# A list schedule's latency towards matmuls, the place of a norm, and the order of small loads in a decoder layer

## The chip, the cores and the metric

The kernel runs on one core of a Trainium2 chip. The metric is the device time of one execution in microseconds (us). One execution of the kernel before was profiled; all rows below come from it. TensorE (PE) does matmuls, PEld stands for its weight loads, VectorE is DVE, ScalarE is ACT, GpSimd is POOL and SyncE is SP; SP issues nearly all DMAs.

## The reference

One decoder layer over 1024 tokens of width 1024, one sequence, float32:

```python
mod = (silu(c) @ w_ada + b_ada)            # shift1, scale1, gate1, shift2, scale2, gate2
h = rms_norm(x, norm1) * (1 + scale1) + shift1
proj = h @ w_in                            # q, k and v of three attention branches, gates, convolution inputs
mix = concat(nsa_attention(...), bgate * conv(cgate * u)) @ w_out
x = x + gate1 * mix
h2 = rms_norm(x, norm2) * (1 + scale2) + shift2
ff = square(relu(h2 @ w_ff1)) @ w_ff2      # width 4096
return x + gate2 * ff
```

The attention has eight heads of 64 and adds three branches (compressed, selected, window), each with its own softmax and a relative-position bias.

## The kernel before

Activations lie transposed: width on the partitions (eight slices, index k or c), tokens along the free axis, in two halves of 512 (hf 0 and 1). For precision each operand of a product is split into a rounded high part and a low rest, and every product is three matmuls (`mm3`): high by high, high by low, low by high. A weight tile is therefore loaded by DMA, cast (`copy`, L336 on ACT, L338 on DVE, L340 on POOL) and subtracted (`sub`, L347) before TensorE can use it. Matmuls are recorded at L312, transposes at L315, `stt` at L358, activations at L330, DMAs at L397.

The program is written twice into a plan: everything up to the second norm is one plan (`P.issue()` after `first_half`, attention and output projection), the MLP is the second. `Plan` collects operations with their costs and dependencies and works out an order by list scheduling in eight passes: `_longest` gives each operation the longest way to the end, `_forward` simulates the engines and the DMA queue and takes, on each engine, the ready operation with the highest priority, and `_backward` gives new priorities from the schedule so found. `LAT` holds the time in ns that passes between an operation on one engine and a dependent one on another. `AHEAD` gives a named group of operations a lead in priority. The order of each engine is the order of the best pass. Within a plan it is fixed; where the second plan's instructions fall among the first's on an engine is left to the framework, so some of the MLP's weight loads are issued before the first plan ends.

The stages, in order of the code:

- The group `silu`: loads of c (`ct`), `ident`, `b_ada` (`bad`) and `norm1` (`n1`), the sigmoid of c, its spread over the partitions (`dg`, two matmuls into `fa_t`, copies to `sc`), and `c1` from `bad` and `n1`. Between them stand the 16 loads of x.
- The first product (groups `stat0`, `stat1`, `first0` to `first7`): squares of x summed by matmuls into `stb` and `po`, `rsqrt_neg2` (three activations, two corrections by `stt`). For each k: two rows of w_ada (512 KB each) are multiplied with silu(c) and accumulated on DVE (128x1024), `a1` comes from that, x is multiplied, scaled and split for both halves, and 18 matmuls (three column groups, two halves, three each) follow, 144 in all.
- Compression, keys, values, queries, tables; then attention in units, with fillers for TensorE: the convolution, the output projection and the norm of the first half (`first_half`), and 30 (`NFF`) of the 32 tiles of w_ff1 for the first half. `put_hid` squares their result in one of five rotating buffers, the cells of `z_t`, `t1_t` and `cg_t`, and stores it to `d_hid` in DRAM.
- The output projection of the second half (`out_proj`, 192 matmuls): `done_second` adds the result to x1 and the squares into `sacc`. Then the second norm: the row sum (matmul into `stb`), `rsqrt_neg2`, and `norm2_apply` for eight k.
- The MLP in four chunks (`ch`) of eight tiles: `load_w` loads and splits a tile of w_ff1 into two rotating buffers `ws_r`; the first half comes from `d_hid` where it is stored and from `ff1(j, 0, w)` where not (tiles 30 and 31, in the last chunk), the second half from `ff1(j, 1, w)`; then w_ff2. A tile of `ff1` is 24 matmuls of 512 columns. Temporaries rotate over four buffers `tmp`.

Of the kernel before, what the change touches and what calls it, by code (L numbers as in the profile page):

```python
# [33 lines left out]
def f32(ap):  # L34
    return ap.bitcast(F)
# [11 lines left out]
class Plan:  # L47
# [6 lines left out]

    PASSES = 8

    LAT = {("ACT", "ACT"): 150, ("ACT", "DVE"): 142, ("ACT", "PE"): 260, ("ACT", "POOL"): 159,
           ("DVE", "ACT"): 128, ("DVE", "DVE"): 127, ("DVE", "PE"): 254, ("DVE", "POOL"): 155,
           ("PE", "ACT"): 197, ("PE", "DVE"): 196, ("PE", "PE"): 0, ("PE", "POOL"): 220,
           ("POOL", "ACT"): 180, ("POOL", "DVE"): 170, ("POOL", "PE"): 203, ("POOL", "POOL"): 102}  # L60

    def __init__(self, tc):
        self.tc, self.nc = tc, tc.nc
# [91 lines left out]
    def _forward(self, prio):  # L155

        ops = self.ops
        prio = [prio[o] for o in ops]
        npred, ready = {o: len(o.preds) for o in ops}, {o: {a[0]: max((t + self._lat(p, o, e, a[0]) for p, e, t in o.past), default=0.0) for a in o.alts} for o in ops}
        free = dict(self.free)  # L160
        heaps, pend = ({e: [] for e in self.eng} for _ in range(2))
        done, order, hw, dma, last, cold, port = bytearray(len(ops)), [], 0.0, 0.0, self.free["PE"], 0.0, 0.0

        def push(o):
            for i, (e, _, _) in enumerate(o.alts):
                heapq.heappush(pend[e], (ready[o][e], prio[o.idx], o.idx, i))

        def arrive(e, t):
            h, p = heaps[e], pend[e]
            while p and p[0][0] <= t:  # L170
                _, pr, idx, i = heapq.heappop(p)
                if not done[idx]:
                    heapq.heappush(h, (pr, idx, i))

        for o in ops:
            if not npred[o]:
                push(o)
        while len(order) < len(ops):
            best = None
            for e in self.eng:  # L180
                h, p = heaps[e], pend[e]
                while h and done[h[0][1]]:
                    heapq.heappop(h)
                while p and done[p[0][2]]:
                    heapq.heappop(p)
                arrive(e, free[e])
                t = free[e] if h else p[0][0] if p else None
                if t is not None and (best is None or t < best[0]):
                    best = (t, e)
            t, e = best  # L190
            free[e] = t
            arrive(e, t)
            if e in ("DVE", "POOL") and port > t:
                h, held = heaps[e], []
                while h and e in ops[h[0][1]].port:
                    held.append(heapq.heappop(h))
                    while h and done[h[0][1]]:
                        heapq.heappop(h)
                first = heapq.heappop(h) if h else None
                for x in held:  # L200
                    heapq.heappush(h, x)
                if first is None:
                    free[e] = min(port, pend[e][0][0]) if pend[e] and pend[e][0][0] > t else port
                    continue
                _, idx, i = first
            else:
                _, idx, i = heapq.heappop(heaps[e])
            o, cost = ops[idx], ops[idx].alts[i][1]
            if e in o.port:
                port = t + cost  # L210
            done[idx] = 1
            if not o.nbytes:
                if e == "PE":
                    if t - last > 2500:
                        cold = t + 4000
                    cost *= 2 if t < cold else 1
                    last = t + cost
                end = free[e] = t + cost
            else:
                if e == "SP":  # L220
                    hw = max(hw, t) + cost
                    start = hw + 650
                else:
                    free[e] = t + cost
                    start = t + cost + 660
                end = dma = max(dma, start) + o.nbytes * o.weight / 360.0
                end += 1000.0
                if e == "SP":
                    free[e] = max(t + 50, hw - cost, dma - 2500)
            order.append((t, o, i, end))  # L230
            for s in o.succs:
                for c in ready[s]:
                    ready[s][c] = max(ready[s][c], end + self._lat(o, s, e, c))
                npred[s] -= 1
                if not npred[s]:
                    push(s)
        return order
# [194 lines left out]


H0, H1, WR, RAN = 0, 8192, 16384, 16384 + 11328
AHEAD = {}
FA1N, FA2N = 13316, 10752

NFF = 30
# [3 lines left out]
def hymba_layer(ctx: ExitStack, tc: tile.TileContext, xT, cT, w_first, w_cols, w_vg, w_ada, w_ada2, b_ada,  # L442
                norm1, norm2, qn, kn, pe, cw1, cw2, conv_w, rel_bias, onehot, ident_c, pair_c, w_out,
                w_ff1, w_ff2, out, dbg=None):
# [32 lines left out]
    d_q = [[dtile(f"d_q{p}{i}", 2, 128, 2, 2, 256) for i in range(2)] for p in range(4)]  # L477
    d_k = [dtile(f"d_k{g}", 128, KW0 + T) for g in range(2)]
    d_v = [dtile(f"d_v{g}", 128, 8, 2, 128) for g in range(2)]
    d_hid = [dtile(f"d_hid{j}", 128, 512) for j in range(NFF)]  # L480
    d_row = dtile("d_row", NH, TROW)
    d_tab = [dtile(f"d_tab{i}", 128, TROW) for i in range(NH)]

# [591 lines left out]
    def first_half():  # L1075

        (ca, t2), (ta, tb) = cg_t, t1_t
        t_r = Rot([z[:, 0:512] for z in z_t] + [t2, tb])

        def done(c, a):  # L1080
            x = x1h[c]
            P.dma(x, xT[c, :, 0:512])
            P.stt(x, a, mod[:, 16 + c:17 + c], x, mult, add)
            add_square(c, ta, ca, x)

        tmp = Rot([ca, ta, tb])
        for k in range(8):
            load_mix(0, k, tmp(), h0[0][:, k], h0[1][:, k])
        tiles = [(w_out[c], lambda a, c=c: done(c, a)) for c in range(8)]
        yield from products([tiles[0:2], *([t] for t in tiles[2:6]), tiles[6:8]], fwx_r, h0)  # L1090
        P.zero(f32(bones), 1.0 / 1024)
        P.dma(n2, norm2)
        P.ts(a2, mod[:, 32:40], 1.0, -0.5, add, mult)
        P.tt(a2, a2, n2, mult)
        st = fa_r()
        P.mm(st, f32(bones), ca, True, True)
        y = rsqrt_neg2(ta, tb, st)
        for k in range(8):
            norm2_apply(k, t_r(), x1h[k], y, h0)
            yield  # L1100
        t_r = Rot(t_r.t + [ca])
        rot = fwx_r

        def put_hid(j, a):
            t = t_r()
            P.act(t, a, AF.Relu)
            P.act(t, t, AF.Square)
            P.dma(d_hid[j], t)

        tiles = [(w_ff1[j], lambda a, j=j: put_hid(j, a)) for j in range(NFF)]  # L1110
        P.group = "ff"
        yield from products([tiles[0:2], *([t] for t in tiles[2:])], rot, h0)

# [44 lines left out]

    x1 = [[FA1[:, 1024 * c + 512 * hf:1024 * c + 512 * hf + 512] for hf in range(2)] for c in range(8)]
    h2 = [h[0], h[1]]  # L1160
    tmp, sacc, y1 = Rot(at0), Gr(512), Gr(512)
    wt_r = Region(RA, RAN - 4160, RAN).rot(4, 2, 512)
    for c in range(8):
        P.dma(x1[c][1], xT[c, :, 512:1024])
# [6 lines left out]
    for k in range(4):  # L1171
        load_mix(1, k, [ada_acc, *ada_r.t][k], h[1][0][:, k], h[1][1][:, k])
    out_proj(wt_r, h[1], Rot(sc_t), done_second)
    P.mm(stb, f32(bones), sacc, True, True)
    rsqrt_neg2(y1, tmp(), stb)
    for k in range(8):
        norm2_apply(k, tmp(), x1[k][1], y1, h[1])
    for c in range(8):
        P.dma(x1[c][0], x1h[c])
    P.issue()  # L1180
# [13 lines left out]
    with ExitStack() as pf:  # L1194
        ff = pool(pf, "ff", side="right")
        psd = pool(pf, "psD", space=PSUM)
        banks = Rot([psd.tile([128, 512], F, name=f"pd{i}") for i in range(8)])
        Fr = Region(FA1, 8192, FA1N)
        ws_r = Fr.rot(2, 8, 128)
        tmp, ff_acc = Fr.rot(4, 512), Fr(512)  # L1200
        w5 = [Region(RA, c, c + 1024)(8, 128) for c in (*range(RAN - 4160, RAN - 1023, 1024), WR)]
        wh_r, wl_r = Rot([w5[0], w5[2], w5[4]]), Rot([w5[1], w5[3]])
        Wr = Region(RA, WR + 1024, RAN - 4160)
# [14 lines left out]
        def ff1(j, hf, w):  # L1218
# [5 lines left out]
            P.act(t, t, AF.Square)  # L1224
            split_hid(j, hf, t)

        for ch in range(4):
            for j in range(8):
                w = load_w(w_ff1[ch * 8 + j])
                if ch * 8 + j < NFF:  # L1230
                    t = tmp()
                    P.dma(t, d_hid[ch * 8 + j])
                    split_hid(j, 0, t)
                else:
                    ff1(j, 0, w)
                ff1(j, 1, w)
            if ch == 0:
                for i in range(2):
                    ada_cols(40 + 4 * i, 4, tmp, ff_acc, banks())
            for c in range(8):  # L1240
                w = load_w(w_ff2[ch, c])
                for hf in range(2):
                    a = banks()
                    for k in range(8):
                        hh = [hid[i][k][hf] for i in range(2)]
                        mm3(a, w, hh, S_[:, k], S_[:], k == 0, k == 7)
                    P.stt(x1[c][hf], a, mod[:, 40 + c:41 + c], x1[c][hf], mult, add)
                    if ch == 3:
                        P.dma(out[c, :, hf * 512:hf * 512 + 512], x1[c][hf])
# [82 lines left out]
```

## Time and profile before

| | |
|---|---|
| median of 3 runs | 1369.71 us (1368.28 to 1371.58) |
| the profiled execution | 1369.85 us |
| its span, first to last instruction | 1368.1 us |
| TensorE busy | 1326.0 us, 97% |
| VectorE busy | 777.8 us, 57% |
| ScalarE busy | 623.2 us, 46% |
| mean granted clock of TensorE | 0.986 |
| read from and written to HBM | 145.48 and 32.61 MB |

The time is a little longer than the span, by what lies around the instructions. Shares are averages over stages that have different limits. TensorE's matmuls are pipelined and their ends are modelled, so TensorE can be shown busy while it runs below its pace: the number of matmuls in a stretch tells more than its busy share.

### The profile page before, as it was taken

What the parts mean: (1) busy time and instruction counts of PE and PEld (TensorE: products, weight loads), DVE (VectorE), ACT (ScalarE), POOL (GpSimd) and SP (SyncE); (2) the same over time, 40 slices, a digit from 0 to 9 for tenths busy, and PEclk for the clock granted to TensorE, in tenths of its full rate; (3) what the DMA queues carried; (4) which work ended last, traced back from release to release, by engine and by line L of the source; (5) the groups of instructions that cost most, each with busy time, mean ns of one, the idle gap of its engine ahead of it and who ended that gap; (6) DMA issues with size and microseconds to landing.
All of it is one profiled execution on the core that took longest, in us unless ns stands there. A gap on an engine that the chain in (4) does not pass through costs nothing.

```text
span 1368.1 us, 18289 instructions
## 1 busy us (share of the span) xinstructions
PE 1326.0 (97%) x6424; PEld 1080.7 (79%) x6424; DVE 777.8 (57%) x1882; ACT 623.2 (46%) x1293; POOL 134.9 (10%) x240
## 2 busy tenths in 40 slices
PE   5899999999999999999999988999999999999998
PEld 2679788887878788888888866888888888888887
DVE  5987886878686886566565557443422442143222
ACT  5766653777564786565666344310320032013200
POOL 0001011332220222121111000000000000000000
PEclk9899999999999999999999998999999999999999
DMA  9468896444252322542325515432322332132131
GB/s 331 149 182 239 234 345 205 157 152 126 71 195 85 100 67 86 174 140 93 109 81 166 166 59 160 135 108 69 116 62 62 92 113 73 32 93 92 39 115 62
DMA packets 91600, 175.62 MB, mean 128 GB/s; under 512 B 10746, under 2 KB 30755, under 8 KB 90997
## 3 DMA queue, kind: packets, MB, share of 16 engines
q1 hardware_dynamic: 87764, 159.65, 37.2%
q0 software_dynamic: 3744, 14.81, 3.4%
q8 instruction: 50, 0.82, 0.3%
q14 instruction: 42, 0.34, 0.1%
HBM read 145.48 MB, written 32.61 MB: 130 GB/s over the span
## 4 chain that ended last, share of the span: by engine, by line
PE 90%; DMA 4%; DVE 4%; ACT 1%; SPq 1%; issue 0%; DVEq 0%; ACTq 0%
PE pd L312 38%; PE fa L312 24%; PE sc L312 16%; PE po L312 7%; PE stb L315 3%; PE sc L315 2%; DVE FA L358 1%; DMA FA<-in_w_ada 1%; DVE FA L347 1%; DMA d_k<-FA 1%; ACT FA L330 1%; SPq L397 1%; DMA FA<-in_cw 1%; DMA d_tab<-d_row 1%; DVE RA L347 1%
## 5 line engine op out<-in xcount | busy, mean ns | idle before, releaser
L312 PE MATMUL fa<-RA 128*128 128x512 f32 (+1 forms) x1384 | 445.7, 409 | 0.5 <-DVE RA L347 0.5
L312 PE MATMUL pd<-RA 128*128 128x512 f32 x1392 | 411.9, 392 | 10.2 <-ACT RA L336 5.6
L336 ACT CAST RA<-FA 128x512 fp32r<-128x512 f32 (+6 forms) x235 | 162.3, 706 | 487.2 <-PE pd L312 292.5
L312 PE MATMUL sc<-RA 128*128 128x512 f32 (+7 forms) x1328 | 354.9, 370 | 14.3 <-DVE RA L338 12.1
L347 DVE TENSOR_TENSOR RA<-FA,RA 128x512 fp32r<-128x512 f32 (+5 forms) x327 | 245.2, 769 | 159.0 <-PE pd L312 92.9
L312 PEld LDWEIGHTS pd<-RA 128*128 128x128 f32 x1392 | 261.4, 189 | 68.1 <-ACT RA L336 6.0
L312 PE MATMUL pd<-hid,RA 128*128 128x512 f32 x960 | 310.5, 389 | 0.0
L312 PEld LDWEIGHTS fa<-RA 128*128 128x128 f32 (+1 forms) x1384 | 248.4, 190 | 43.2 <-DVE RA L347 1.6
L312 PEld LDWEIGHTS sc<-RA 128*128 128x128 f32 x1328 | 237.1, 191 | 57.4 <-DVE RA L338 13.1
L312 PEld LDWEIGHTS pd<-hid,RA 128*128 128x128 f32 x960 | 180.2, 188 | 37.5
L358 DVE SCALAR_TENSOR_TENSOR FA<-pd,mod,FA 128x512 f32<-128x512 f32 x64 | 46.4, 746 | 199.5 <-PE pd L312 199.5
L312 PE MATMUL po<-RA 128*128 128x256 f32 (+2 forms) x564 | 139.8, 303 | 1.4 <-DVE RA L347 1.4
L330 ACT ACTIVATE FA<-FA,nm 128x64 f32<-128x64 f32 (+5 forms) x192 | 114.7, 600 | 18.1 <-DVE nm L366 17.7
L312 PEld LDWEIGHTS po<-RA 128*128 128x128 f32 (+1 forms) x564 | 101.8, 191 | 12.9 <-ACT RA L336 1.7
L377 DVE CUSTOM_DVE_ANT_0 FA<-sc,FA 128x64 f32<-128x64 f32 (+5 forms) x192 | 84.8, 455 | 40.6 <-PE sc L312 39.2
L330 ACT ACTIVATE FA<-FA 128x512 f32<-128x512 f32 (+2 forms) x147 | 88.9, 619 | 24.3 <-DVE FA L358 12.3
L370 POOL TENSOR_SCALAR FA<-FA,cf 128x64 f32<-128x64 f32 (+8 forms) x109 | 73.0, 681 | 163.3 <-DVE cf L347 130.5
L315 PE MATMUL stb<-FA,FA 128*128 128x128 f32 (+1 forms) x304 | 74.8, 275 | 0.3 <-DVE RA L347 0.3
L347 DVE TENSOR_TENSOR RA<-stb,RA 128x512 fp32r<-128x512 f32 (+1 forms) x84 | 53.3, 635 | 36.4 <-PE po L312 17.8
L315 PE MATMUL sc<-FA,FA 128*128 128x128 f32 (+1 forms) x288 | 69.8, 277 | 0.0
L347 DVE TENSOR_TENSOR RA<-sc,RA 128x512 fp32r<-128x512 f32 (+2 forms) x84 | 51.0, 607 | 25.9 <-ACT RA L336 21.4
L336 ACT CAST RA<-stb 128x512 fp32r<-128x512 f32 (+1 forms) x84 | 45.2, 538 | 40.6 <-PE stb L315 39.7
(124 smaller groups left out, 908.8 us busy)
## 6 DMA issues: line engine op xcount, KB each, us to landing
FA<-in_w_ff SPq DMA_DIRECT2D x64, 512.0 KB, 4.3
FA<-in_w_ada SPq DMA_DIRECT2D x64, 256.0 KB, 3.2
FA<-in_w_ff SPq DMA_DIRECT2D x60, 256.0 KB, 2.7
FA<-in_w_cols SPq DMA_DIRECT2D x34, 256.0 KB, 3.7
FA<-in_xT SPq DMA_DIRECT2D x32, 256.0 KB, 5.4
FA<-in_w_ada SPq DMA_DIRECT2D x16, 512.0 KB, 7.1
d_q<-FA SPq DMA_DIRECT2D x32, 256.0 KB, 4.5
RA<-d_q POOLq DMA_DIRECT2D x16, 512.0 KB, 4.6
```

The source lines that it names most:

```text
L312: self.op([("PE", c, lambda: self.nc.tensor.matmul(out, a, b, start=start, stop=stop))], [out], [a, b])
L315: self.op([("PE", 110.0, lambda: self.nc.tensor.transpose(out, a, ident))], [out], [a, ident])
L330: self.op([("ACT", c, lambda: self.nc.scalar.activation(out, a, func, **kw))], outs, ins)
L336: alts.append((e, 0.833 * n + (53 if ps else 93), lambda: self.nc.scalar.copy(out, a)))
L347: alts.append((e, 1.04 * n + 68, lambda: self.nc.vector.tensor_tensor(out, a, b, op)))
L358: self.op([("DVE", 1.04 * self._n(out) + 68 + 61 * ptr, lambda: self.nc.vector.scalar_tensor_tensor(out, a, s, b, op0, op1, **kw))], [out] ...
L370: alts.append((e, 0.833 * n + 174 + 83 * ptr, lambda: self.nc.gpsimd.tensor_scalar(out, a, s1, s2, op0, op1)))
L377: self.op([("DVE", 1.04 * self._n(out) + 75, lambda: self.nc.vector.tensor_tensor_reduce(out, a, b, 1.0, init, ALU.add, ALU.max, accum))], ...
L397: self.op([(q, c, lambda: e.dma_start(out=out, in_=a))], [out], [a], nbytes=n, weight=2 if within else 1)
```

## The change

Three things, and no instruction is added or dropped:

- `LAT` from ACT, DVE and POOL to PE grows by 600 ns, and the simulated DMA rate falls from 360 to 320 bytes per ns in `_forward`.
- The group `silu` gets a lead of 30000 ns in priority.
- The second norm of the second half moves from the first plan to the head of the MLP's plan, and the tiles of w_ff1 that the fillers compute are now 2 to 31 in place of 0 to 29, so that tiles 0 and 1 are computed in the MLP. `sacc` becomes `t1_t[1]`, the MLP's fourth `tmp` and `ff_acc` (which is also `y1`) move to the end of `FA1`.

```diff
-    LAT = {("ACT", "ACT"): 150, ("ACT", "DVE"): 142, ("ACT", "PE"): 260, ("ACT", "POOL"): 159,
-           ("DVE", "ACT"): 128, ("DVE", "DVE"): 127, ("DVE", "PE"): 254, ("DVE", "POOL"): 155,
+    LAT = {("ACT", "ACT"): 150, ("ACT", "DVE"): 142, ("ACT", "PE"): 860, ("ACT", "POOL"): 159,
+           ("DVE", "ACT"): 128, ("DVE", "DVE"): 127, ("DVE", "PE"): 854, ("DVE", "POOL"): 155,
            ("PE", "ACT"): 197, ("PE", "DVE"): 196, ("PE", "PE"): 0, ("PE", "POOL"): 220,
-           ("POOL", "ACT"): 180, ("POOL", "DVE"): 170, ("POOL", "PE"): 203, ("POOL", "POOL"): 102}
+           ("POOL", "ACT"): 180, ("POOL", "DVE"): 170, ("POOL", "PE"): 803, ("POOL", "POOL"): 102}
...
-                end = dma = max(dma, start) + o.nbytes * o.weight / 360.0
+                end = dma = max(dma, start) + o.nbytes * o.weight / 320.0
...
-AHEAD = {}
+AHEAD = {"silu": 30000}
...
-        tiles = [(w_ff1[j], lambda a, j=j: put_hid(j, a)) for j in range(NFF)]
+        tiles = [(w_ff1[j], lambda a, j=j: put_hid(j, a)) for j in range(32 - NFF, 32)]
...
-    tmp, sacc, y1 = Rot(at0), Gr(512), Gr(512)
+    tmp, sacc = Rot(at0), t1_t[1]
...
-    P.mm(stb, f32(bones), sacc, True, True)
-    rsqrt_neg2(y1, tmp(), stb)
-    for k in range(8):
-        norm2_apply(k, tmp(), x1[k][1], y1, h[1])
...
-        Fr = Region(FA1, 8192, FA1N)
+        Fr, Gr = Region(FA1, 8192, FA1N - 1536), Region(FA1, FA1N - 1024, FA1N)
         ws_r = Fr.rot(2, 8, 128)
-        tmp, ff_acc = Fr.rot(4, 512), Fr(512)
+        tmp, ff_acc = Rot([*Fr.rot(3, 512).t, Gr(512)]), Gr(512)
...
+        st, y1 = banks(), ff_acc
+        P.mm(st, f32(bones), sacc, True, True)
+        rsqrt_neg2(y1, tmp(), st)
+        for k in range(8):
+            norm2_apply(k, tmp(), x1[k][1], y1, h[1])
         for ch in range(4):
             for j in range(8):
                 w = load_w(w_ff1[ch * 8 + j])
-                if ch * 8 + j < NFF:
+                if ch * 8 + j >= 32 - NFF:
```

## Rows read from the trace of the kernel before

**Rows 1.** The page: busy us of each engine (share of the span) xinstructions.
```profile
PE 1326.0 (97%) x6424; PEld 1080.7 (79%) x6424; DVE 777.8 (57%) x1882; ACT 623.2 (46%) x1293; POOL 134.9 (10%) x240
```
**Rows 2.** Stages: length, busy us (xinstructions) of each engine, TensorE's clock, DMA share, GB/s.
```profile
20.00:41.00 21.00, 5.76 (x9) 1.84 (x8) 19.86 (x42) 7.57 (x13) 0.33 (x3) 0.70 0.98 354
41.00:60.00 19.00, 19.00 (x75) 15.56 (x76) 19.00 (x41) 16.69 (x30) 0.30 (x2) 0.89 0.30 92
...
240.00:760.00 520.00, 517.49 (x2842) 424.87 (x2841) 362.29 (x1126) 342.87 (x814) 116.92 (x195) 1.00 0.38 122
...
811.00:827.00 16.00, 5.85 (x18) 3.37 (x18) 12.67 (x23) 12.61 (x20) 0.00 (x0) 0.78 0.29 98
...
960.00:1060.00 100.00, 100.00 (x442) 82.06 (x441) 32.54 (x45) 21.74 (x29) 0.00 (x0) 1.00 0.26 79
```
**Rows 3.** Timeline of the start: start us, us, engine line operation [idle before, releaser].
```profile
9.34 0.17 DVE L366 TENSOR_SCALAR sl<-ct 128x8 f32<-128x8 f32 x1 [7.84 <-DMA ct<-in_cT]
...
16.32 1.22 DVE L358 SCALAR_TENSOR_TENSOR FA<-FA 128x1024 f32<-128x1024 f32 x1 [2.77 <-ACT FA L336]
...
16.96 0.69 ACT L330 ACTIVATE FA<-stb,eps 128x512 f32<-128x512 f32 x1
...
25.92 0.43 SPq L397 DMA_DIRECT2D n<-in_norm  x1
...
37.37 0.16 DVE L367 TENSOR_SCALAR n<-n 128x8 f32<-128x8 f32 x1
...
41.00 1.22 PE L312 MATMUL sc<-RA 128*128 128x512 f32 x2 [12.10 <-DVE RA L338]
```
**Rows 4.** Stretches of low clock, columns as in rows 2.
```profile
41.00:45.20 4.20, 4.20 (x10) 3.33 (x11) 4.20 (x10) 4.20 (x8) 0.00 (x0) 0.50 0.95 306
...
814.80:826.10 11.30, 1.15 (x4) 0.38 (x3) 11.23 (x21) 9.63 (x15) 0.00 (x0) 0.73 0.35 116
826.10:830.30 4.20, 4.20 (x10) 3.33 (x11) 4.02 (x7) 1.41 (x2) 0.00 (x0) 0.50 0.39 105
...
92.00:96.00 4.00, 2.06 (x11) 1.23 (x10) 3.80 (x7) 2.95 (x5) 0.00 (x0) 1.00 0.78 270
96.50:99.80 3.30, 3.30 (x13) 2.74 (x13) 3.21 (x6) 2.98 (x8) 0.99 (x1) 0.50 0.61 192
```
**Rows 5.** Timeline behind the output projection, columns as in rows 3.
```profile
808.06 1.22 DVE L347 TENSOR_TENSOR RA<-FA,RA 128x1024 fp32r<-128x1024 f32 x1
...
811.15 5.33 SPq L397 DMA_DIRECT2D d_hid<-FA  x2
...
815.49 0.63 ACT L330 ACTIVATE FA<-FA 128x512 f32<-128x512 f32 x1
...
818.17 9.83 SPq L397 DMA_DIRECT2D FA<-in_w_ff  x3
...
825.01 2.50 ACT L336 CAST RA<-FA 128x1024 fp32r<-128x1024 f32 x3
```
**Rows 6.** DMA issues: operation xcount, KB each, median us from issue to landing.
```profile
FA<-in_w_ff SPq DMA_DIRECT2D x64, 512.0 KB, 4.3
...
d_hid<-FA SPq DMA_DIRECT2D x2, 256.0 KB, 2.0
```
**Rows 7.** Timeline of VectorE where the first product ends, columns as in rows 3.
```profile
60.19 5.69 DVE L347 TENSOR_TENSOR RA<-FA,RA 128x512 fp32r<-128x512 f32 x10
...
68.60 2.61 DVE L338 COPY FA<-sc 64x512 f32<-64x512 f32 x4 [2.40 <-ACT FA L336]
```
**Rows 8.** Matmuls by form, 240 to 760 us: xcount | busy us, mean ns | idle before.
```profile
L312 PE MATMUL fa<-RA 128*128 128x512 f32 x1135 | 371.7, 415 | 0.5 <-DVE RA L347 0.5
L312 PE MATMUL po<-RA 128*128 128x256 f32 x514 | 129.6, 302 | 0.0
L312 PE MATMUL sc<-RA 128*128 128x512 f32 x278 | 108.2, 420 | 1.7 <-DVE mx L377 1.7
L315 PE MATMUL stb<-FA,FA 128*128 128x128 f32 x280 | 68.5, 275 | 0.3 <-DVE RA L347 0.3
```

More of the change, by code (lines that the diff above doesn't have):

```diff
@@ L479, in hymba_layer @@
     d_v = [dtile(f"d_v{g}", 128, 8, 2, 128) for g in range(2)]
-    d_hid = [dtile(f"d_hid{j}", 128, 512) for j in range(NFF)]
+    d_hid = [dtile(f"d_hid{j}", 128, 512) for j in range(32)]
     d_row = dtile("d_row", NH, TROW)
```

## The prediction

> **What bounds the kernel now.** I read the page first: TensorE is busy 97% of the span [rows 1], so only time in which TensorE waits, or runs below its pace, can be won. Next I read the stage table, to see where that time lies. The pace is the stage at 960 to 1060 us: 442 matmuls of 512 columns in 100 us, 0.226 us each, at a granted clock of 1.00 [rows 2]. Against it three places fall short: the start (up to 41 us TensorE has only the statistics to do and is busy 5.76 of the last 21 us), the stretch 811 to 827 us (busy 5.85 of 16 us), and, less plainly, 240 to 760 us [rows 2]. The timelines of the first two tell which wait ends last there, the rows by form how much is hidden in the third, and the table of clocks what an idle stretch costs after it has ended.
>
> At the start the first product matmul begins at 41.00 and had waited for a cast of the normed x. That cast needs a1, which needs c1, which needs norm1 and b_ada; norm1's load is issued only at 25.92, behind the loads of x and w_ada, and its first use comes at 37.37, with accumulations of w_ada queued ahead of it on VectorE [rows 3]. At 811 us the second half's norm chain (row sum, Ln, Exp, two corrections, eight applications) stands between the output projection and the first MLP tile, and only what is left of the fillers covers it. In the MLP itself (960 to 1060) nothing is lost.
>
> **The sum is made against the profiled execution**: span 1368.1, time 1369.85, so 1.75 lie outside the span; the median of the runs is 1369.71, 0.14 off, and the result below stands for either.
>
> **Part 1: the second norm moves into the MLP's plan, and the two w_ff1 tiles without a stored first half become tiles 0 and 1 instead of 30 and 31.** No instruction is added: two tiles of 24 matmuls leave the last chunk and run while the norm chain runs. What goes away: between 814.8 and 826.1 TensorE is idle 11.30 - 1.15 = 10.15 us, and its next 4.20 us run at a clock of 0.50, so half of them, 2.1 us, is lost too [rows 4]. Together 12.25. The cover offered is 48 x 0.226 = 10.9 us. What is late next is the weights. Tile 0's were split by 808.06 + 1.22 = 809.3 [rows 5] and are ready. Tile 1's staging buffer overlaps the temporary of the last filler tile, so its load waits for that tile's store: the last square at 815.49, its store behind it, the load at 818.17, casts from 825.01 [rows 5]. Unchanged, tile 1 would start near 825.3, while tile 0 ends at 814.8 + 5.4 = 820.2: 5.1 us idle and about 2.1 at half clock, gain 12.25 - 7.2 = 5. But the last filler is no longer wanted behind the projection, and tile 28's buffer is now the accumulator of the row sums, which forces that tile ahead of the projection's first result. If the last filler ends 3 us before the projection, its store lands about when the projection ends (two activations of 0.63 [rows 5], store 2.0 [rows 6]); the load of 4.3 [rows 6], a cast of about 1 and a subtraction of 1.22 [rows 5] give tile 1's weights some 7 us behind the projection, against 6 to 6.5 us of cover (tile 0 and the row sum): 1 us lost, and perhaps 1 at a lower clock. I take **10**, between 5 and 12.25. That the norm chain's temporaries are now shared with the MLP's delays only the reads of finished products from PSUM: there are eight banks, and nothing else needs those products before eight tiles are through. The last chunk loses 10.9 us of matmuls and gets two more loads of 256 KB; its transfers (rate about 80 GB/s now in the MLP [rows 2]) hide them.
>
> **Part 2: the small loads first (a lead of 30 us for their group in the list).** Four issues of 0.43 us [rows 3] go ahead of x: 1.7 us of SP's queue, paid by the first statistics. The first statistics end at 16.96 [rows 3]; with 1.7 later, 3.4 for Ln, Exp, Square and two corrections (0.69 each, as Ln [rows 3]), about 2.0 for product, scaling and cast, and one or two 1.2 us accumulations in the way on VectorE, the first product matmul comes at 25 to 27 instead of 41.00. That is not the gain. VectorE is busy 19.86 of 21 us and then 19.00 of 19 [rows 2], and its work for this stage is unchanged: per k two accumulations (2 x 1.22 [rows 3]), four passes over 512 columns (half of 1.22 for 1024 [rows 5]), one over 384 and small ones, about 5.8 us, while TensorE needs 18 x 0.226 = 4.1 us. So TensorE starts early and then follows VectorE. VectorE itself can begin sooner only by what the c load now costs it: its first operation waited 7.84 us for it, and the first accumulation at 16.32 waited 2.77 us for the scaled c [rows 3]; but then w_ada has to be there, at a DMA share of 0.98 [rows 2]. Say 0 to 3 us. What VectorE also gets back is its idle time behind TensorE's backlog, 2.40 us at 68.60 [rows 7]. TensorE's own bound is the whole wait, 12.1, plus half of 4.20 us at clock 0.50 [rows 3, 4]: 14.2. Nearest to the limiting engine is the VectorE bound, 0 to 5.4; TensorE's backlog lets some more through, since the 144 matmuls would end some 4 us behind VectorE's last pass for this stage (about 62, within [rows 7]), at 66, instead of at 41.00 + 144 x 0.226 = 73.6. I take **6**, between 0 and 13.
>
> The Trainium skill speaks against such a move: "DMA: Bandwidth & Descriptors", Rules for kernel authors, says that transfers under 64 KB are mostly overhead. The rows show that overhead as issue time alone, 0.43 us each, and by them it is in the sum; had the rule meant whole landing times in series, the sum would be some 5 us worse.
>
> **Part 3: 600 ns more from any engine to TensorE, and 320 instead of 360 bytes per ns for DMA.** Both change the model, so only the order of the same instructions. A matmul is put later behind what it reads, and ready ones go between. What this can win is idle time that comes from late producers: about 1.9 us at 92 us and half of 3.30 at clock 0.50 after it [rows 4], one of three such places before 480 us, together about 10. At this one VectorE is busy 3.80 of 4.00 us [rows 4], so it is the bound and not the order; I take **2**. What it can lose lies at 240 to 760: of 2842 matmuls the four largest groups, 1135 x 512, 514 x 256, 278 x 512 and 280 x 128 columns, take 394 us at 0.226 us per 512 columns, the other 635, mostly 128 columns, about 35 more, and the stretch has 520 [rows 2, 8]. So some 90 us (an estimate) go where matmuls of different kinds follow each other. A new order may change that by 5% either way without any reason that I could name: -5 to +10 for this part.
>
> Sum: 10 + 6 + 2 = 18; 1369.85 - 18 = **1352**.
>
> **The rivals.** (a) *The start gives nothing that lasts.* VectorE and the DMAs carry the stage, TensorE runs dry between the k, and each dry spell costs clock as at 41 to 45.2, where it stood at 0.50 [rows 4]. For it: VectorE's load. Against: the backlog that VectorE waited for at 68.60. Gain 10 + 0 + 2: 1358.
>
> The Trainium skill has this as a rule, "TensorE: Matmul & The Clock Gate", HAM oscillation: waits that recur leave the engine slow each time. Here the trace agrees for single waits (0.50 after 92 us as well); a stage that oscillates is in no run yet.
>
> (b) *The start pays in full and the three small stalls go too*: 12 + 13 + 4 = 29, 1341. For it: TensorE has 12.1 us of plain waiting there. Against: VectorE.
>
> (c) *The change doesn't do what it says at the norm.* The MLP's TensorE order puts tiles 0 and 1 behind the row sum and the norm, or tile 1's weights come as late as now. Gain 0 to 5 there: 1357 to 1362, 1360 as one figure.
>
> (d) *Slower: the new order breaks up the attention's matmuls.* Place: 240 to 760. Price: 0.9 us for each per cent by which the 90 us grow. From 20% more (18 us) it eats the forecast's gain, and from 23% the kernel is slower by over 0.2%, at 1373 or above. For it: a longer way makes attention's steps wait in the model, so more filler matmuls are put between them. Against: the number of instructions of each kind is unchanged, and the 90 us would have to grow by a fifth while no group gets more instructions.
>
> **How the numbers follow.** 0.2%, 2.7 us, is about what a measurement of this kernel can tell from no change. Chances: the forecast, 1345 to 1359, 0.60; (a) 0.14; (b) 0.10; (c) 0.08; (d) 0.05 for slower, and 0.03 for something between that ends within 0.2%. So faster 0.92, same 0.03, slower 0.05. The range reaches from (b) to the late end of (c): 1342 to 1363. It leaves out half of (b), (d) and what ends within 0.2%, with the edges of the others less than 2 in 10.
>
> **What would show it.** Part 1: TensorE busy nearly throughout the 15 us behind the output projection, 24 to 48 MLP matmuls ahead of the first that reads the second half's h, no half clock there. Tile 1's weight load issued before the projection ends; if it is issued after, 5 us are lost again. Part 2: c, norm1 and b_ada loaded in the first 3 us, the first product matmul at 25 to 27 with short waits between the k, the 144th at about 66 instead of 74, and VectorE free of first-stage work no more than 3 us sooner. Part 3: as many matmuls in an attention stretch of 520 us as now, within 2%. The prediction is wrong if the time from the start to the middle of the attention falls by over 12 us or not at all, or if the attention itself gets longer or shorter by over 5 us.

## The result, and the profile after

The changed kernel takes 1353.28 us (median of 4, 1352.0 to 1355.87) where the kernel before takes 1370.64 beside it: ratio 0.988, interval 0.986 to 0.990. The profiled execution is 1352.0 with a span of 1350.2, 17.9 less than before's; it is the fastest of the four. A second measurement gave 0.986 (0.985 to 0.988).

The stage table of the changed kernel, columns as in [rows 2]; the third line is the boundary to the MLP (the 16 us behind the output projection's end), the fourth the MLP's steady stage, and the last two are the end of the start:

```profile
20.00:41.00 21.00, 13.95 (x32) 6.98 (x33) 20.97 (x43) 12.37 (x22) 0.33 (x3) 0.84 0.93 332
...
240.00:760.00 520.00, 516.35 (x2809) 424.32 (x2808) 354.44 (x1059) 329.38 (x757) 104.70 (x180) 0.99 0.38 122
...
805.50:821.50 16.00, 12.65 (x52) 9.14 (x51) 12.50 (x20) 10.47 (x16) 0.00 (x0) 1.00 0.36 110
...
955.00:1055.00 100.00, 100.00 (x443) 82.81 (x442) 31.82 (x43) 22.42 (x29) 0.00 (x0) 1.00 0.26 79
...
32.40:41.00 8.60, 6.39 (x20) 4.36 (x21) 8.60 (x17) 3.89 (x8) 0.00 (x0) 0.80 0.77 249
41.00:72.00 31.00, 31.00 (x134) 24.02 (x133) 28.50 (x63) 24.78 (x47) 0.53 (x4) 1.00 0.47 147
```

At the boundary 52 matmuls run in 16 us, where there were 18 in the 16 us of [rows 2], and the clock stands at 1.00 instead of 0.78. The steady MLP has its 443 matmuls in 100 us as before. The attention's stretch holds as many matmuls as before within 1.2% (2809 against 2842 [rows 2]); counted by their columns, it holds as much within 0.2% (1951 against 1948 matmuls of 512 columns, summed over the forms). At the start 20 product matmuls are begun by 41 us, when the first began before.

The clock at the boundary isn't the same in every execution. In a second profiled execution of the changed kernel ("again" in the table below) 3.4 us of it run at 0.50:

```profile
808.50:811.90 3.40, 3.06 (x5) 1.83 (x6) 0.20 (x1) 0.94 (x2) 0.00 (x0) 0.50 0.80 293
```

To divide the gain without trusting busy shares, take the last transposition, which ends the attention. Its start is the last number of these rows of the transpose line (operation, count, durations in ns, first and last start in the stretch from 400 us; shapes), in the kernel before:

```profile
L315 PE MATMUL stb<-FA,FA x215: 270/272/332, 399.7 to 760.0; 128*128 128x128 f32 x104, 128*64 128x128 f32 x4
```

in the changed kernel:

```profile
L315 PE MATMUL stb<-FA,FA x204: 270/272/421, 401.4 to 751.7; 128*128 128x128 f32 x98, 128*64 128x128 f32 x4
```

with part 1 alone:

```profile
L315 PE MATMUL stb<-FA,FA x217: 270/272/421, 400.0 to 761.9; 128*128 128x128 f32 x104, 128*64 128x128 f32 x5
```

and with part 2 alone:

```profile
L315 PE MATMUL stb<-FA,FA x208: 270/272/332, 435.4 to 756.2; 128*128 128x128 f32 x100, 128*64 128x128 f32 x4
```

Up to there the changed kernel is 8.3 us ahead (751.7 against 760.0). From there to the end of the span it takes 1350.2 - 751.7 = 598.5 us against 1368.1 - 760.0 = 608.1, 9.6 less. So in these two executions the gain falls into two almost equal halves: the way to the attention's end, and the boundary to the MLP. For every kernel below I give both parts, the front and the back. The cut is a fair one: in every kernel 3806 to 3814 of the 6424 matmuls have begun by that transposition.

The timeline of the boundary in the changed kernel, columns as in [rows 3], to be read against [rows 5]:

```profile
803.61 2.20 PE L312 MATMUL sc<-RA 128*128 128x512 f32 x9
...
805.09 0.33 SPq L397 DMA_DIRECT2D d_hid<-FA  x1
...
807.10 12.00 SPq L397 DMA_DIRECT2D FA<-in_w_ff  x3
...
808.57 1.10 PE L312 MATMUL pd<-FA,bones 128*128 128x512 f32 x2 [2.76 <-DVE FA L347]
...
809.10 5.96 PE L312 MATMUL pd<-RA 128*128 128x512 f32 x22
...
811.63 1.03 ACT L336 CAST RA<-FA 128x1024 fp32r<-128x1024 f32 x1
...
815.58 19.79 PE L312 MATMUL pd<-RA 128*128 128x512 f32 x86 [0.52 <-DVE RA L338]
```

The projection's last matmuls end at 805.81. The row sum (bones) stands first and TensorE waits 2.76 for it, then come 22 MLP matmuls, a pause of 0.52 for VectorE's cast of the normed h, and 86 without a pause. The last filler's store goes out at 805.09, tile 1's load follows at 807.10, 1.3 us behind the projection, and its cast comes at 811.63, some 6 us behind it.

The start, from the timeline of the changed kernel:

```profile
1.65 0.43 SPq L397 DMA_DIRECT2D n<-in_norm  x1
...
2.45 0.17 DVE L366 TENSOR_SCALAR sl<-ct 128x8 f32<-128x8 f32 x1 [0.94 <-DMA ct<-in_cT]
...
2.60 3.75 SPq L397 DMA_DIRECT2D FA<-in_xT  x8
...
13.65 1.23 DVE L358 SCALAR_TENSOR_TENSOR FA<-FA 128x1024 f32<-128x1024 f32 x1 [6.19 <-DMA FA<-in_w_ada]
...
16.81 0.67 ACT L330 ACTIVATE FA<-stb,eps 128x512 f32<-128x512 f32 x1
...
25.27 1.37 SPq L397 DMA_DIRECT2D FA<-in_w_first  x3
...
31.94 1.34 ACT L336 CAST RA<-FA 128x384 fp32r<-128x384 f32 x3
...
32.49 1.16 PE L312 MATMUL sc<-RA 128*128 128x512 f32 x2 [2.60 <-ACT RA L336]
...
55.98 5.71 DVE L347 TENSOR_TENSOR RA<-FA,RA 128x512 fp32r<-128x512 f32 x10
...
63.46 2.61 DVE L338 COPY FA<-sc 64x512 f32<-64x512 f32 x4 [1.45 <-ACT FA L336]
```

The small loads are issued by 2.55 us, VectorE's first accumulation starts at 13.65 instead of 16.32 and now waits for w_ada itself, and VectorE's last passes of the stage start at 55.98 instead of 60.19 [rows 7]. The end of the first product is read from the third column group, whose 48 matmuls (the first `fa<-RA` ones) include the last of the 144. Its row gives the count, the durations in ns, and the first and last start; in the kernel before:

```profile
L312 PE MATMUL fa<-RA x48: 388/389/628, 42.0 to 76.7; 128*128 128x512 f32 x48
```

in the changed kernel:

```profile
L312 PE MATMUL fa<-RA x48: 388/389/628, 33.4 to 70.5; 128*128 128x512 f32 x48
```

So the product starts 8.5 us sooner and ends 6.2 us sooner.

### The profile page after: what moved, and what is told of

It reads as the page before. It is cut to its first block, busy times and chain, and to the rows that moved or that the text cites. A ratio compares the mean times of both kernels' runs of the same rounds, so it can differ in the third digit from the quotient of the medians.

```text
span 1350.2 us, 18276 instructions
## 1 busy us (share of the span) xinstructions
PE 1322.4 (98%) x6424; PEld 1079.6 (80%) x6424; DVE 776.7 (58%) x1882; ACT 626.6 (46%) x1294; POOL 131.5 (10%) x239
## 4 chain that ended last, share of the span: by engine, by line
PE 88%; DVE 6%; DMA 3%; issue 1%; ACT 1%; SPq 0%; POOL 0%; DVEq 0%; ACTq 0%; POOLq 0%
PE pd L312 39%; PE fa L312 23%; PE sc L312 15%; PE po L312 6%; PE stb L315 3%; PE sc L315 2%; DVE FA L358 2%; DVE RA L347 1%; DVE FA L347 1%; ACT FA L330 1%; DVE FA L377 1%; DMA FA<-in_w_ada 1%; DMA d_tab<-d_row 0%; SPq L397 0%; DMA d_k<-FA 0%
## 5 line engine op out<-in xcount | busy, mean ns | idle before, releaser
L336 ACT CAST RA<-FA 128x512 fp32r<-128x512 f32 (+5 forms) x237 | 163.8, 707 | 459.0 <-PE pd L312 273.0
L347 DVE TENSOR_TENSOR RA<-FA,RA 128x512 fp32r<-128x512 f32 (+5 forms) x327 | 248.9, 777 | 141.0 <-PE pd L312 68.4
L330 ACT ACTIVATE FA<-FA,nm 128x64 f32<-128x64 f32 (+6 forms) x192 | 114.9, 601 | 24.4 <-DVE nm L366 23.7
L370 POOL TENSOR_SCALAR FA<-FA,cf 128x640 f32<-128x640 f32 (+8 forms) x115 | 72.6, 642 | 238.5 <-DVE cf L347 136.2
L315 PE MATMUL stb<-FA,FA 128*128 128x128 f32 (+1 forms) x304 | 76.7, 279 | 3.0 <-DVE RA L347 3.0
L347 DVE TENSOR_TENSOR RA<-sc,RA 128x512 fp32r<-128x512 f32 (+2 forms) x84 | 51.1, 608 | 25.5 <-ACT RA L336 14.4
L336 ACT CAST RA<-sc 128x512 fp32r<-128x512 f32 (+2 forms) x84 | 43.6, 519 | 38.3 <-PE sc L315 35.3
```

What stands on the lines that cost most here:

```text
L315: self.op([("PE", 110.0, lambda: self.nc.tensor.transpose(out, a, ident))], [out], [a, ident])
L330: self.op([("ACT", c, lambda: self.nc.scalar.activation(out, a, func, **kw))], outs, ins)
L336: alts.append((e, 0.833 * n + (53 if ps else 93), lambda: self.nc.scalar.copy(out, a)))
L347: alts.append((e, 1.04 * n + 68, lambda: self.nc.vector.tensor_tensor(out, a, b, op)))
L370: alts.append((e, 0.833 * n + 174 + 83 * ptr, lambda: self.nc.gpsimd.tensor_scalar(out, a, s1, s2, op0, op1)))
```

## The experiments

Each is timed against the kernel before on the same chip, and the ratios are to that: its median was 1370.64 beside the changed kernel and 1371.96, 1372.32 and 1372.05 beside the three groups of four that follow in the table. Front and back are those of each kernel's profiled execution; a front varies by several us between executions of one order (shown below), a back by about one.

| kernel | median us | ratio (interval) | front us | back us |
|---|---|---|---|---|
| before | 1370.64 | 1 | 760.0 | 608.1 |
| changed | 1353.28 | 0.988 (0.986 to 0.990) | 751.7 | 598.5 |
| part 1 alone | 1364.22 | 0.995 (0.993 to 0.997) | 761.9 | 599.0 |
| part 2 alone | 1367.05 | 0.996 (0.995 to 0.997) | 756.2 | 609.0 |
| latency alone | 1369.35 | 0.998 (0.997 to 0.999) | 758.2 | 607.1 |
| latency and rate (part 3) | 1371.93 | 1.000 (0.999 to 1.002) | 764.9 | 607.8 |
| parts 1 and 2 | 1358.31 | 0.990 (0.988 to 0.991) | 756.8 | 599.6 |
| parts 2 and 3 | 1360.85 | 0.991 (0.990 to 0.993) | 753.0 | 607.0 |
| parts 1 and 3 | 1363.12 | 0.994 (0.993 to 0.995) | 765.4 | 599.0 |
| changed, first weight early | 1357.24 | 0.989 (0.988 to 0.991) | 755.9 | 598.1 |
| changed, again | 1352.70 | 0.986 (0.985 to 0.988) | 752.0 | 599.4 |
| changed, 590 ns | 1356.66 | 0.989 (0.988 to 0.991) | 754.6 | 598.1 |
| changed, 610 ns | 1354.45 | 0.988 (0.986 to 0.990) | 754.5 | 598.4 |
| changed, tile 0 ahead of the row sum | 1357.08 | 0.989 (0.987 to 0.991) | 756.8 | 600.4 |

**Each part alone.** Part 1 alone is the kernel before with the hunks on the norm, the tiles and the buffers:

> The kernel before with part 1 alone: second norm in the MLP's plan, tiles 2 to 31 by the fillers. Theory (parts add up, this one is worth about 10): 1360.5, TensorE idle for under 4 us between the output projection and the MLP and no half clock there; the stretch up to 240 us as before within 3 us. Rival (the norm's cover depends on the longer latency, because without it the plan puts the row sum and the norm first): 1365 or more, with an idle stretch of over 5 us at that place.

Measured: 1364.22, 7.3 us less by the ratio. The back is 9.1 us shorter, and its boundary is the changed kernel's, matmul for matmul in number, without any longer latency:

```profile
814.50:830.50 16.00, 12.65 (x52) 9.04 (x50) 12.50 (x20) 10.28 (x16) 0.00 (x0) 1.00 0.32 98
```

So the cover doesn't depend on part 3. The front came out 1.9 longer; its order is another, since tiles 2 to 31 and the shared buffer change the first plan too, and two executions of one order can differ by more (below).

Part 2 alone:

```diff
-AHEAD = {}
+AHEAD = {"silu": 30000}
```

> The kernel before with part 2 alone: a lead of 30 us for the small loads' group. Theory: about 6 us less, 1364.5, first product matmul at 27 to 33 us instead of 41, the gain complete by 240 us and nothing changed behind it but a shift. Rival (VectorE and the DMAs carry the start, nothing lasts): 1369 to 1371 with the first product matmul just as early. Rival (it needs the longer latency or the slower DMA rate to last): gain under 3.

Measured: 1367.05, 5.2 us less by the ratio. First product matmul at 30.60, front 3.8 us shorter, back 0.9 longer. At the same number of matmuls it is 3.7 to 4.0 us ahead of the kernel before from 160 us to the attention's end, so the gain is complete by then, as the theory has it. The rival that nothing of the start lasts falls; by its size the gain is between the theory's 6 and the third view's 3.

Part 3, first the latency alone, then with the rate:

```diff
-    LAT = {("ACT", "ACT"): 150, ("ACT", "DVE"): 142, ("ACT", "PE"): 260, ("ACT", "POOL"): 159,
+    LAT = {("ACT", "ACT"): 150, ("ACT", "DVE"): 142, ("ACT", "PE"): 860, ("ACT", "POOL"): 159,
...
-                end = dma = max(dma, start) + o.nbytes * o.weight / 360.0
+                end = dma = max(dma, start) + o.nbytes * o.weight / 320.0
```

> The kernel before with 600 ns more from ACT, DVE and POOL to PE, nothing else. Theory: 2 us less, 1368.5, from the short stalls between 80 and 160 us. Rival (the whole gain of the start is this one's, the small loads are a by-product): 1364 or less. Rival (orders only get worse in the attention): 1373 or more, with fewer matmuls in 520 us of attention.

> As the last, with the simulated DMA rate at 320 too. Theory: as that one within 2 us, 1368.5. Rival (the rate matters where DMAs carry the work, up to 200 us): 3 us or more less than that one.

Measured: 3.0 us less with the latency, nothing (1.000) with both. The first product matmul stays at 41.80 and 41.17: the start is not this part's. The attention holds 2825 and 2808 matmuls in its 520 us. For the latency alone the theory's 2 us are about met and no rival holds; that they come from the stalls between 80 and 160 us is not shown. With the rate, theory and rival both miss: the slower simulated DMA took back 2.6 us, and the two intervals don't touch.

**All but one part.** If the parts added up, 0.995, 0.996 and 1.000 would give 0.991; the whole is at 0.986 to 0.988.

> The changed kernel without the longer latency and with the simulated DMA rate at 360 again: parts 1 and 2 alone. The two alone took 7.3 and 5.2 us off. Theory (parts add up): 12 to 13 us under the kernel before, so the model's numbers bring the remaining 4 of the whole change. Rival (the two parts help each other and the model's numbers are worth nothing, as alone): 16 us or more under it.

Measured: 0.990, 14.4 us less: between the theory's 12 to 13 and the rival's 16, both within its interval, and 2 to 4 short of the whole.

> The changed kernel with the second norm and the tiles as before: parts 2 and 3. Theory (parts add up; the model's numbers alone gave 0): 5 us under the kernel before. Rival (the model's numbers help the start only together with the early small loads): 8 us or more under it.

Measured: 0.991, 11.8 us less, the rival's number. Parts 2 and 3, 5.2 and 0 alone, have a front 7 us shorter together. The back is 607.0, with the idle boundary again:

```profile
808.00:824.00 16.00, 7.67 (x20) 4.62 (x19) 13.11 (x23) 12.21 (x18) 0.00 (x0) 0.68 0.31 97
```

> The changed kernel without the lead of the small loads: parts 1 and 3. Theory (parts add up): 7 to 8 us under the kernel before, and the place of the norm looks as with part 1 alone. Rival (the longer latency puts the MLP's tiles better around the norm): 10 us or more under it, with less idle time between the output projection and the MLP than with part 1 alone.

Measured: 0.994, 8.4 us less: the theory's number. The boundary is part 1's, with 599.0 behind the attention, and the front is no better than before's.

So part 1 is worth about 9 us in the back whatever stands beside it (608.1, 609.0, 607.1, 607.8 and 607.0 without it, 598.1 to 600.4 with it), and part 3 is worth nothing without part 2's early loads and 2 to 7 us with them (16.4 to 18.6 less 14.4, and 11.8 less 5.2). The orders in the traces bear out that the parts can be told apart this way. Parts 2 and 3 together run in the changed kernel's order on every engine up to 740 us; part 3 runs in one order with and without part 1 up to 753 us, and part 2 up to 495 us. Where one of the others is there, adding part 1 hardly touches the front; it shortens the back by 7.6 to 9.4 us (by the ratios: 9.2 beside part 2, 8.4 beside part 3, 4.6 to 6.8 beside both).

**The first matmul earlier.** In the changed kernel the start's last wait is a weight. This one loads that weight first:

```diff
+    P.group = "w0"
+    ws0 = wfs_r()
+    P.dma(ws0, w_first[0])
...
-        ws = wfs_r()
-        P.dma(ws, w_first[k])
+        if k:
+            ws = wfs_r()
+            P.dma(ws, w_first[k])
+        else:
+            ws = ws0
```

with a lead of 15 us for the group `w0`.

> The changed kernel with the first k's weight tile of the first product loaded right behind the small loads and ahead of x. In the changed kernel the first product matmul waited at 32.49 for that weight's cast, whose load was issued at 25.27 behind w_ada. Theory (VectorE carries the start, so an earlier first matmul is not the gain): first product matmul at 25 to 27, the time 0 to 2 us under the changed kernel. Rival (TensorE's start is what counts): 4 us or more under it, 1349 or less.

Measured: 1357.24, a ratio of 0.989: neither the rival's 4 us less nor the theory's 0 to 2, but level with the changed kernel or slower. TensorE starts 8 us sooner, and its stretches up to 72 us, VectorE's last passes of the stage and the third column group show what becomes of it:

```profile
24.40:41.00 16.60, 10.06 (x22) 5.92 (x23) 16.07 (x31) 9.39 (x15) 0.10 (x1) 0.71 0.92 334
41.00:72.00 31.00, 31.00 (x129) 24.54 (x128) 28.54 (x63) 23.77 (x45) 0.53 (x4) 0.96 0.44 123
...
57.72 5.70 DVE L347 TENSOR_TENSOR RA<-FA,RA 128x512 fp32r<-128x512 f32 x10
...
L312 PE MATMUL fa<-RA x48: 388/389/628, 25.0 to 72.5; 128*128 128x512 f32 x48
```

Six of the first 22 are still statistics, so only 16 product matmuls are begun by 41 us, against 20 in the changed kernel, which starts 8 us later. VectorE is busy 16.07 of 16.60 us: TensorE starts early and then follows it, at a lower clock (0.71). The last product matmul comes at 72.5, 2.0 us later than in the changed kernel, and VectorE's last passes start at 57.72, 1.7 later: the weight now stands ahead of x and w_ada, and VectorE's first accumulation starts at 15.77 instead of 13.65. So the end of the product moved with VectorE and against TensorE's first matmul. That the first matmul is not the start's bound is shown by this run.

**The order by itself.** Two kernels differ from the changed one by 10 ns of latency, which says nothing new about the chip but gives other orders; the changed kernel ran beside them once more.

> The changed kernel once more, as the measure for the three beside it on one chip. 0.988 of the kernel before, as in its first measurement, within 0.002.

> The changed kernel with 590 ns added to the latency instead of 600: a change that means nothing for what the model knows, but gives another order. Theory (which of several equally good orders the passes end in is worth several us, and that is why the parts don't add up): differs from the changed kernel by 2 to 5 us either way. Rival (the extra ns themselves are worth something): within 1 us of it.

> As the last with 610 ns. Theory (order alone): 2 to 5 us away from the changed kernel or from the one with 590. Rival (the ns themselves): within 1 us of both.

Measured: 0.986, 0.989 and 0.988; the medians are 4.0 and 1.8 us above the changed kernel's beside them, and the intervals overlap. So these runs don't show whether such an order is worth anything: the next kernel's median lies 4.4 us above too, though its order is the changed kernel's up to the boundary and its back only 1 to 2 us longer. But what part 3 brings beside parts 1 and 2 is no larger than this, so that the longer latency as such brings it is not shown either.

**The row sum's wait.** The changed kernel's largest wait at the boundary is 2.76 us ahead of the row sum. This one tells the MLP's plan that three engines are free sooner:

```diff
+        for e in ("SP", "ACT", "DVE"):
+            P.free[e] -= 8000.0
         st, y1 = banks(), ff_acc
```

> The changed kernel with ScalarE, VectorE and SyncE taken as free 8 us sooner when the MLP's plan begins, so that 13 matmuls of its tile 0 stand ahead of the row sum. In the changed kernel the row sum stood first and TensorE was idle 2.76 us for it. Theory: the wait goes, 2 to 3 us less than the changed kernel. Rival (the norm is late by as much and the wait comes back at the first matmul that reads the second half's h): within 1 us of the changed kernel, with an idle stretch of 2 us or more some 10 us later.

Measured: 1357.08, not faster. The wait went and came back, as the rival has it. TensorE's timeline there, and the 16 us from 810.5:

```profile
810.69 0.61 PE L312 MATMUL pd<-RA 128*128 128x512 f32 x2
811.46 2.80 PE L312 MATMUL pd<-RA 128*128 128x512 f32 x11 [0.16 <-DVE RA L347]
814.10 1.02 PE L312 MATMUL pd<-FA,bones 128*128 128x512 f32 x2
814.55 3.07 PE L312 MATMUL pd<-RA 128*128 128x512 f32 x11
818.96 0.73 PE L312 MATMUL pd<-RA 128*128 128x512 f32 x2 [1.34 <-ACT RA L336]
821.83 2.66 PE L312 MATMUL pd<-RA 128*128 128x512 f32 x5 [2.14 <-DVE RA L338]
...
810.50:826.50 16.00, 12.36 (x43) 8.52 (x42) 11.29 (x18) 9.09 (x14) 0.00 (x0) 0.89 0.28 87
```

The 13 matmuls run first, the row sum stands at 814.10 instead of 808.57, and TensorE then waits 1.34 for tile 1's weights and 2.14 for the normed h; the clock falls too, to 0.89 over these 16 us, with 43 matmuls instead of 52. By these waits the boundary is limited by the norm chain and tile 1's weights together, not by the row sum's place; the back is 600.4, 1 to 2 us longer than the changed kernel's.

The order of this kernel is that of the changed kernel up to the boundary, and yet its front is 756.8 where the changed kernel's two executions have 751.7 and 752.0. From 60 to 160 us it has 498 matmuls in 100 us,

```profile
60.00:160.00 100.00, 94.60 (x498) 79.50 (x497) 78.82 (x186) 62.01 (x137) 9.52 (x17) 0.98 0.79 219
```

where the changed kernel's execution has 513:

```profile
60.00:160.00 100.00, 97.92 (x513) 82.07 (x512) 82.30 (x193) 65.41 (x144) 10.46 (x19) 0.98 0.81 234
```

Instruction for instruction, this execution falls behind by 2 us up to 75 us and by 5 up to 150, and from there to the attention's end stays 5.0 to 5.7 behind. Parts 2 and 3, of the same order, have 753.0. So the front of one execution is not a measure of an order to better than 5 us. The medians are a better one, but where four runs stand behind them not to better than some 3 us: here the median is 4.4 above the changed kernel's with 1 to 2 us in the back.

## Why the prediction was right, step by step

**The total.** 1352 was predicted, 1352.0 profiled, 1353.28 the median. The three terms were 10, 6 and 2, and the profile gives 9.6 behind the attention's end and 8.3 ahead of it. That the sum is so close is partly chance: fronts of one order differ by 5 us, the profiled execution is the fastest of four, and the third term is not shown (below).

**Part 1: 10 forecast, 9.6 in the profile, 9 with the others taken away.** The mechanism is the one worked out: MLP matmuls in the norm's shadow, tile 1's weights some 6 us behind the projection because the last filler was done by its end. What was lost in [rows 4] is gone but for 2.76 + 0.52 us of waiting and, in the second execution, 3.4 us at a clock of 0.50 (at most half of them lost). Three details were wrong. The 2 us were to be lost at tile 1's weights, but most of the loss lies ahead of the row sum, which the plan puts first: the wait of 2.76 for the projection's last sum stands in no term. Of the 48 covering matmuls only 22 stand ahead of the first that waits for the normed h, where 24 to 48 were named as the sign; the other 26 fall among those that read h, and TensorE runs on without a pause. And tile 1's load was issued 1.3 us behind the projection, which by the prediction's sign should have cost 5 us again; it didn't, as its cast was done by 812.66, when only 13 of the 22 had run.

**Part 2: 6 forecast, 5.2 alone.** Its bound, VectorE, was right, and the early first matmul was rightly not taken for the gain. Several sizes were off. The first product matmul was to come at 25 to 27 and came at 32.49: the step that failed is the chain that I followed, from the statistics through VectorE, which left out the weight of the first k. The new order itself had put that weight back: its load was issued at 25.27, behind w_ada, where the kernel before issues its first such load at 15.78. Its cast at 31.94 was the last to come. The run that loads it first has the matmul at 24.44, so the rest of that chain held. VectorE's lead in this stage was to be at most 3 us and is 4.2 (55.98 against 60.19). And the 144 matmuls were to end 8 us sooner, at 66 instead of 74; the last begins 6.2 us sooner, at 70.5 instead of 76.7. The prediction's 73.6 for the kernel before left out what the 4.20 us at half clock cost, which it counts elsewhere [rows 4].

The issue time of the four small loads is 0.39 to 0.43 each as forecast, and x is delayed by it: its first load goes at 2.60, before at 0.75. But the first statistics didn't pay the 1.7 us that the sum charges them: their Ln starts at 16.81, before at 16.96 [rows 3]. The Trainium skill ("DMA: Bandwidth & Descriptors", Rules for kernel authors) says that under 64 KB one pays mostly overhead. The 4 KB of c, issued at 0.75 and read 1.7 us later, agree with that. It decides nothing here: the four loads are issued one behind the other in 1.8 us, ahead of everything, and whole landing times in series, which the prediction priced at 5 us, aren't seen.

**Part 3: 2 forecast, 0 alone, 2 to 7 beside part 2.** The short stalls that it was to cure are partly gone: from 72 to 160 us TensorE has 464 matmuls and 85.92 busy us of 88 instead of 436 and 83.64. From 60 to 160 us the kernels with part 2 but not part 3 have 481 and 488 matmuls, those with both, in the changed kernel's order, 498 to 513. Against that, a stall grew: a wait of 3.0 for VectorE ends at 486 us, where the longest before was 1.7. The row of TensorE's waits:

```profile
PE stb L315 <- DVE RA L347: 3.0, 1, 3.0
```

And the two stretches between 72 us and the end of the MLP that run at a clock of 0.50, columns as in [rows 2]:

```profile
145.30:148.60 3.30, 3.30 (x11) 2.66 (x10) 3.27 (x7) 2.67 (x7) 0.00 (x0) 0.50 0.99 337
486.60:493.30 6.70, 6.70 (x26) 5.28 (x23) 6.61 (x18) 6.64 (x16) 0.00 (x0) 0.50 0.00 0
```

VectorE is busy 6.61 of 6.70 us in the second, and the wait ahead of it ends a chain that lies on VectorE from 479.8 us on, so VectorE is the bound there. How much of what part 3 wins up to 160 us lasts to the attention's end the fronts can't tell. As the runs with 590 and 610 ns differ from the whole by about as much as part 3 does, I can't say that the forecast's 2 us were right for their reason.

**The rivals.** (a) and (c) are refuted by parts 2 and 1 alone. (d) is refuted: the kernel is faster, and in no kernel does the attention's count of matmuls in 520 us fall by more than 1.3% (2805 at the least, with parts 1 and 3, against 2842 before [rows 2]). Even that is mostly a change of sizes: counted by columns every kernel's 520 us hold 1944 to 1960 matmuls of 512, before 1948. Nor did the attention get longer or shorter by 5 us: the lead is 6.2 us at the end of the first product and 8.3 at the attention's end. (b) asked for TensorE's start to pay in full; the run with the early weight shows that it doesn't. The rule of the Trainium skill beside (a), that recurring waits leave TensorE slow ("TensorE: Matmul & The Clock Gate", HAM oscillation), shows in part: up to 41 us the product runs at 0.80 in the changed kernel and at 0.71 with the early weight, but from there to 72 us the clock is 1.00 and 0.96.

**What stays open.** Which of the two numbers of part 3 helps beside part 2, and whether it is more than a lucky order. No version that beats the changed kernel was found: the two that were meant to remove its last waits at the start and at the boundary are level with it or slower. The cause of the spread between executions of one order is open too.

## What to carry to other kernels

A chain that stands between two stages of the bounding engine is best covered by work of the later stage that doesn't read the chain's result: here moving two tiles cost nothing that the runs show and held its 8 to 9 us with every other part changed. When a small load feeds a long queue, put it first, but price the move by the engine that limits the stage and not by the first instruction of the engine that waits; and follow every operand of that instruction, weights too. In a kernel whose order a program searches for, changes of a few us need a control that changes the order alone, one that repeats the same order, and more than four runs of each.

## What the runs showed that I had not expected

Two executions of one order, up to the boundary, differ by 5 us in their front (751.7 and 756.8), all of it by 160 us; from 60 to 160 us the DMA share is 0.79 and 0.81, against 0.38 in the attention, where the two keep step. What the spread comes from is not shown. And it is as large as the 4 us by which 10 ns in a model's latency moved the median, which is why that move can't be read.
